# A mixture of experts: two sums of the experts' rows in DRAM in turn, an earlier place for their readback, one accumulation for the last two tiles, and the router in column halves

## The chip, the cores and the metric

The kernel runs on one core of a Trainium2 chip. A core has a matrix engine (TensorE, called PE in the profile), a vector engine (VectorE, DVE), a scalar engine (ScalarE, ACT), a general engine (GpSimd, POOL) and a synchronisation engine (SyncE, SP) that mostly issues transfers. Each has its own queue of instructions, worked off in order. Sixteen DMA engines move data between DRAM and the on-chip memory (SBUF); matmul results land in PSUM. The metric is the device time of one execution in microseconds.

## What is computed

512 tokens of 1024 numbers pass a first block (a state space branch and a pooling branch, then a mixture of experts) and a second block (a linear recurrent layer and differential attention). The change touches the mixture of experts alone:

```python
u2 = modulate(rmsnorm(h, norm_ffn_g), sh2, sc2)
h = h + g2[:, None, :] * moe_ffn(u2, ...)
# moe_ffn
scores = sigmoid(uf @ w_router)               # 512 x 64
choice = scores + router_bias                 # best 4 of 8 groups, then best 8 experts
wts = scores[top_e] / sum * 2.5
# every expert e on the tokens that chose it, and a shared expert on all:
#   (silu(u @ we_gate[e]) * (u @ we_up[e])) @ we_down[e], weighted, summed per token
```

All weights come from DRAM in 32 bits: 3 MB for one expert, 65 experts with the shared one.

## The kernel before

`moe` makes the block. The residual stream `hT` lies in SBUF with features in partitions. `modulated` norms it and makes eight operands u of 128x512 by a product on DVE (L325) and a scale and shift, on ACT (L329) or DVE (L331) in turn; `on_u` multiplies each with the router's weights into one PSUM tile (`logit`, L794); the rows of u are stored to DRAM as `u2_d`. `Routing.run` turns the logits (L855 to L859), picks the experts and sorts them by their counts.

`Schedule` then lists 52 tiles of 128 slots: four of the shared expert, 22 of one expert, 10 third tiles and 16 with two experts that take 64 columns each. `Experts.run` works through them. For a tile, POOL gathers 128 rows of `u2_d` by an indirect DMA (`fetch`, m_xg, L1164), PE turns them (L1179), multiplies gate and up (L1191), ACT and DVE make the hidden rows (m_hid), PE turns these (L1208, evicted to m_ht) and multiplies down (L1191, PSUM tag mm, three buffers). ACT and DVE evict the two halves with the weights of the slots into m_y (L1231, L1233; five buffers of 128x1024). For the shared tiles, a plain DMA writes m_y to `rt_d` (L1237); for others an indirect DMA adds its rows to `rt_d` by the token number (L1242), once for a tile of one expert, twice for one of two (index lists sgi and sgj): 66 such scatters. Since all add to one tensor, each waits until the last one has landed, and the buffer m_y is not free before. POOL issues gathers and scatters in one queue, in the order of the program.

SP issues the weights into m_we and m_wl (nine and six buffers of 1 MB), up to five experts ahead.

The last two tiles (`t.add`) aren't scattered. `parts` splits their rows in two float32r parts (L1258, L1259), `added` multiplies these by a one-hot matrix (`to`) into features by tokens (L1272, L1273), and `residual` (L1263) adds the product to `hT`. `back` reads `rt_d` when all scatters have landed (L1285, issued by SP), PE transposes it (L1290), and `residual` adds it. One `added` stands ahead of the last down product, the other after a loop over further blocks that these inputs don't need. There `on_h` feeds the sums of the next norm (`nsum`, L1424) as each part of `hT` is finished.

Of the kernel before, what the change touches and what calls it, by code (L numbers as in the profile page):

```python
# [166 lines left out]
class K:  # L167
# [142 lines left out]
    def modulated(self, pool, x, inv, gname, sh, sc, uh=None, ul=None, u_cb=None, rows=None, tile=None):  # L310
# [6 lines left out]
        for h in range(2):  # L317
# [5 lines left out]
            for k in range(4 * h, 4 * h + 4):  # L323
# [3 lines left out]
                if u_cb:  # L327
                    if k % 2:
                        nc.scalar.activation(u, u, AF.Identity, scale=a, bias=b)  # L329
                    else:  # L330
                        nc.vector.tensor_scalar(u, u, a, b, op0=OP.mult, op1=OP.add)  # L331
                    u_cb(k, u)
                    continue
# [428 lines left out]
def moe(g, hT, inv, on_h=None):  # L762
# [8 lines left out]
    rt_d = g.dram.tile([512, 1024], F32, name="rt_d")  # L771
    with contextlib.ExitStack() as st:
# [6 lines left out]
        with tc.tile_pool(name="head", bufs=1, reuse_waits="tile") as sp:  # L779
# [8 lines left out]
            with tc.tile_pool(name="route", bufs=1, reuse_waits="tile") as s3:  # L788
# [3 lines left out]
                def on_u(k, u):  # L792
                    us[k] = u
                    nc.tensor.matmul(logit[:64], lhsT=wr[:, k * 64:(k + 1) * 64], rhs=u, start=k == 0, stop=k == 7)  # L794
# [22 lines left out]
class Routing:  # L817


    def __init__(self, g, rp):  # L820
# [20 lines left out]
        nc.vector.tensor_scalar(self.half[:, 2:3], self.half[:, 0:1], 4096.0, None, op0=OP.mult)  # L841
        nc.gpsimd.memset(self.cap, 128.0)
# [3 lines left out]
    def run(self, sp, logit, rb, gc, store):  # L846
# [7 lines left out]
        lg = x[:64]  # L854
        nc.scalar.activation(lg, logit[:64], AF.Copy)  # L855
        p = sm()
        for c in range(4):
            first = nc.tensor.transpose(p[:, 64 * c:64 * c + 64], lg[:, c * P:(c + 1) * P], g.ident[:64, :64]).ins
# [261 lines left out]
class Experts:  # L1120
    def __init__(self, g, wp, lp, xp, u2_d, rt_d, hT):
        self.g, self.wp, self.lp, self.xp, self.u2_d, self.rt_d, self.hT = g, wp, lp, xp, u2_d, rt_d, hT
        self.raw, self.xg, self.us = {}, {}, []
# [28 lines left out]
    def begin(self):  # L1152

        self.raw = {i: self.load(e, i) for i, e in enumerate((64, 0, 1))}

# [65 lines left out]
    def out(self, tl, t):  # L1221
# [14 lines left out]
        if not tl.key:  # L1236
            nc.gpsimd.dma_start(out=self.rt_d[tl.b * P:tl.b * P + P], in_=y)  # L1237
        else:

            to = self.sl(tl.key)  # L1240
            for ix in (to[0],) if len(tl.ws) == 1 else (to[0][:64], to[2]):
                nc.gpsimd.indirect_dma_start(  # L1242
                    out=self.rt_d, out_offset=bass.IndirectOffsetOnAxis(ap=ix, axis=0), in_=y[:ix.shape[0]], in_offset=None,
                    bounds_check=511, oob_is_err=False, compute_op=OP.add)

    def parts(self, tl, t):
# [4 lines left out]
        to = self.tile("to", 512, 2, F32R)  # L1251
# [14 lines left out]
    def added(self, on_h=None):  # L1266

        yh, yl, to = self.add.pop(0)
        for m in range(8):
            p = self.g.acc()  # L1270
            s = slice(m * P, m * P + P)
            self.g.nc.tensor.matmul(p, lhsT=yh[:, s], rhs=to, start=True, stop=False)  # L1272
            self.g.nc.tensor.matmul(p, lhsT=yl[:, s], rhs=to, start=False, stop=True)  # L1273
# [6 lines left out]
    def back(self):  # L1280

        g, nc = self.g, self.g.nc
        tok = [self.x_tile().rearrange("p (c f) -> p c f", c=4) for q in range(4)]
        for q in range(4):
# [1179 lines left out]
```

## Time and profile before

| | us |
|---|---|
| median of 3 runs | 2569.54 (2568.93 to 2570.04) |
| profiled execution, its own time | 2574.54 |
| its span, from first to last instruction | 2572.8 |
| PE busy in the span | 2298.5 (89%) |
| DVE, ACT, POOL busy | 1308.7, 872.6, 759.6 |
| mean granted clock of PE | 0.949 |

Busy shares are means over stages that differ. A time in brackets behind a row is how long the engine sat idle before it, with an arrow to what it waited for. "L1242" is line 1242 of the kernel before. A tile's name stands without its buffer number: m_y is any of five buffers.

### The profile page before, as it was taken

The numbers are of one execution on the slowest core, as the hardware profiler recorded it, in microseconds if no ns is written. First come the engines' busy times: TensorE is split into PE (matmuls) and PEld (weight loads), VectorE is DVE, ScalarE is ACT, GpSimd is POOL, SyncE is SP. The second block draws the span as 40 slices with busy tenths as digits, with TensorE's granted clock in tenths as the row PEclk, the third lists the DMA queues.
The fourth block names the chain that finished last, engine by engine and source line by source line (L and its number), as shares of the span: only waits on it lengthen the run. The fifth ranks groups of instructions, "written<-read, shape, count | busy, mean of one in ns | idle before, by whom it ended". The sixth has DMA issues, their size and how long they took to land. (4 is left out here: it accounts for less than half of the span.)

```text
span 2572.8 us, 31633 instructions
## 1 busy us (share of the span) xinstructions
PE 2298.5 (89%) x11908; PEld 1646.4 (64%) x11908; DVE 1308.7 (51%) x2391; ACT 872.6 (34%) x1593; POOL 759.6 (30%) x589
## 2 busy tenths in 40 slices
PE   6899999998998999797888884898989999989997
PEld 2677888776885544333333333676778798888887
DVE  5666778658544433111111123858634557478765
ACT  3443433343222211111111111645315654345552
POOL 2333344013000121121212122538613311655212
PEclk9899999999998999899999996899989999999998
DMA  7223332345625799899899963376756342111221
GB/s 279 91 98 107 107 107 90 115 164 186 227 94 213 247 328 390 307 332 371 284 398 346 341 201 110 99 204 183 214 139 228 133 161 92 55 55 54 87 66 50
DMA packets 186602, 472.97 MB, mean 184 GB/s; under 512 B 62269, under 2 KB 113853, under 8 KB 146256
## 3 DMA queue, kind: packets, MB, share of 16 engines
q1 hardware_dynamic: 161392, 422.38, 45.9%
q0 software_dynamic: 15712, 35.12, 5.7%
q10 hardware_dynamic: 9344, 13.44, 1.7%
q8 instruction: 94, 1.54, 0.2%
q14 instruction: 60, 0.49, 0.1%
HBM read 421.56 MB, written 69.80 MB: 191 GB/s over the span
## 5 line engine op out<-in xcount | busy, mean ns | idle before, releaser
L224 POOL TENSOR_TENSOR wl<-wr,wh 128x1024 fp32r<-128x1024 f32 x80 | 203.7, 2562 | 384.7 <-ACT wh L223 382.1
L223 ACT ACTIVATE wh<-wr 128x1024 fp32r<-128x1024 f32 (+1 forms) x202 | 204.2, 1043 | 228.6 <-PE mm L205 147.2
L205 PE MATMUL mm<-uh,wh 128*128 128x512 f32 x640 | 258.7, 405 | 10.4 <-DVE cv L607 7.7
L205 PE MATMUL mm<-ul,wh 128*128 128x512 f32 x640 | 256.4, 401 | 0.0
L205 PE MATMUL mm<-uh,wl 128*128 128x512 f32 x640 | 255.7, 400 | 0.0
L205 PE MATMUL mm<-ya,wh 128*128 128x256 f32 x1280 | 242.8, 290 | 7.1 <-ACT wh L223 7.1
L1191 PE MATMUL mm<-m_we,m_x 128*64 128x512 f32 (+1 forms) x672 | 247.8, 599 | 0.0
L205 PEld LDWEIGHTS mm<-ya,wh 128*128 128x128 f32 x1280 | 203.8, 195 | 14.2 <-ACT wh L223 8.7
L224 DVE TENSOR_TENSOR wl<-wr,wh 128x1024 fp32r<-128x1024 f32 (+1 forms) x122 | 157.7, 1311 | 66.3 <-ACT wh L223 66.1
L205 PE MATMUL mm<-ya,wl 128*128 128x256 f32 x640 | 184.2, 288 | 0.0
L1191 PE MATMUL mm<-m_we,m_ht 128*64 128x512 f32 (+1 forms) x368 | 148.7, 621 | 28.0 <-ACT m_y L1231 23.4
L1191 PE MATMUL mm<-m_wl,m_x 128*64 128x512 f32 (+1 forms) x432 | 166.8, 598 | 2.9 <-DVE m_y L1233 1.8
L1242 POOL DMA_INDIRECT rt_d<-m_y,sgi x46 | 70.3, 1528 | 334.4 <-ACT m_y L1231 132.7
L1191 PEld LDWEIGHTS mm<-m_we,m_x 128*64 128x64 f32 (+1 forms) x672 | 86.7, 160 | 101.0 <-issue 99.6
L205 PEld LDWEIGHTS mm<-uh,wh 128*128 128x128 f32 x640 | 122.5, 191 | 41.6 <-issue 8.1
L1181 DVE COPY m_x<-sm 128x512 f32<-128x512 f32 x48 | 33.1, 690 | 223.2 <-PE mm L1191 171.0
L205 PEld LDWEIGHTS mm<-ul,wh 128*128 128x128 f32 x640 | 122.1, 191 | 29.1 <-issue 0.3
L205 PEld LDWEIGHTS mm<-uh,wl 128*128 128x128 f32 x640 | 121.9, 190 | 29.3
L205 PEld LDWEIGHTS mm<-ya,wl 128*128 128x128 f32 x640 | 124.7, 195 | 0.5
L1233 DVE TENSOR_SCALAR m_y<-mm,ssw 128x512 f32<-128x512 f32 x46 | 34.4, 749 | 162.4 <-DMA rt_d<-m_y,sgj 82.6
L1191 PE MATMUL mm<-m_wl,m_ht 128*64 128x512 f32 (+1 forms) x216 | 90.3, 634 | 28.6 <-ACT m_y L1231 20.0
L1191 PEld LDWEIGHTS mm<-m_wl,m_x 128*64 128x64 f32 (+1 forms) x432 | 57.7, 158 | 82.9 <-issue 76.2
(573 smaller groups left out, 4921.5 us busy)
## 6 DMA issues: line engine op xcount, KB each, us to landing
m_we<-in_w_exp_dram SPq DMA_DIRECT2D x117, 1024.0 KB
m_wl<-in_w_exp_dram SPq DMA_DIRECT2D x78, 1024.0 KB
wr<-in_w_grp_dram SPq DMA_DIRECT2D x32, 1024.0 KB
wr<-in_w_ada_dram SPq DMA_DIRECT2D x18, 1024.0 KB
ck<-pk_d SPq DMA_DIRECT2D x16, 1024.0 KB
csb<-cs_d ACTq DMA_DIRECT2D x16, 512.0 KB
wr<-in_w_pg_dram SPq DMA_DIRECT2D x8, 1024.0 KB
raw<-in_w_ada_dram SPq DMA_DIRECT2D x6, 1024.0 KB
```

The costliest lines, as they stand in the source:

```text
L205: nc.tensor.matmul(pt, lhsT=l, rhs=r, start=n == 0, stop=n == last)
L223: self.nc.scalar.activation(hi, src, AF.Copy)
L224: return (eng or self.nc.vector).tensor_sub(lo, src, hi.bitcast(F32)).ins
L1181: nc.vector.tensor_copy(x[:, 4:], v_(p, 4))
L1191: self.mark = self.g.nc.tensor.matmul(p[s], lhsT=x[:, s], rhs=w, start=start, stop=stop).ins
L1233: nc.vector.tensor_scalar(y[:, s], p, w, None, op0=OP.mult)
L1242: nc.gpsimd.indirect_dma_start(out=self.rt_d, out_offset=bass.IndirectOffsetOnAxis(ap=ix, axis=0), in_=y[:ix.shape[0]], in_offset=None, bo ...
```

## The change

The sum in DRAM becomes two, `rt_d[0]` and `rt_d[1]`, to which the scatters add in turn (`turn`); the shared tiles write the first, and `begin` clears the second from a zeroed m_y with four plain DMAs on POOL's queue. `back` reads both in two column halves (four transfers of 1 MB into m_we tiles), adds them with DVE and POOL, and then transposes; it stands ahead of the last tile's turn in the program. The `added` of the tile before the last is gone as a step of its own: `added(on_h)` accumulates both tiles, four matmuls for a part of 128 features instead of two. In the router all eight scales and shifts are ACT's, the logit product writes even k to partitions 0 to 63 and odd k to 64 to 127, and the four transposes of logits become matmuls with two identities on top of each other (`two`), which add the halves.

```diff
@@ modulated
-                    if k % 2:
-                        nc.scalar.activation(u, u, AF.Identity, scale=a, bias=b)
-                    else:
-                        nc.vector.tensor_scalar(u, u, a, b, op0=OP.mult, op1=OP.add)
+                    nc.scalar.activation(u, u, AF.Identity, scale=a, bias=b)
@@ moe
-    rt_d = g.dram.tile([512, 1024], F32, name="rt_d")
+    rt_d = [g.dram.tile([512, 1024], F32, name="rt_d%d" % i) for i in range(2)]
...
-                    nc.tensor.matmul(logit[:64], lhsT=wr[:, k * 64:(k + 1) * 64], rhs=u, start=k == 0, stop=k == 7)
+                    o = 64 * (k % 2)
+                    nc.tensor.matmul(logit[o:o + 64], lhsT=wr[:, k * 64:(k + 1) * 64], rhs=u, start=k < 2, stop=k > 5)
@@ Routing
+        self.two = t([P, 64], "two")
+        nc.vector.tensor_add(self.two, g.ident[:, :64], g.ident[:, 64:])
...
-        lg = x[:64]
-        nc.scalar.activation(lg, logit[:64], AF.Copy)
+        nc.scalar.activation(x, logit, AF.Copy)
         p = sm()
         for c in range(4):
-            first = nc.tensor.transpose(p[:, 64 * c:64 * c + 64], lg[:, c * P:(c + 1) * P], g.ident[:64, :64]).ins
+            first = nc.tensor.matmul(p[:, 64 * c:64 * c + 64], lhsT=x[:, c * P:(c + 1) * P], rhs=self.two, start=True,
+                                     stop=True).ins
@@ Experts.begin
+        zero = self.y()
+        self.g.nc.gpsimd.memset(zero, 0.0)
+        for b in range(4):
+            self.g.nc.gpsimd.dma_start(out=self.rt_d[1][b * P:b * P + P], in_=zero)
@@ Experts.out
-            nc.gpsimd.dma_start(out=self.rt_d[tl.b * P:tl.b * P + P], in_=y)
+            nc.gpsimd.dma_start(out=self.rt_d[0][tl.b * P:tl.b * P + P], in_=y)
...
+                self.turn ^= 1
                 nc.gpsimd.indirect_dma_start(
-                    out=self.rt_d, out_offset=bass.IndirectOffsetOnAxis(ap=ix, axis=0), in_=y[:ix.shape[0]], in_offset=None,
+                    out=self.rt_d[self.turn], out_offset=bass.IndirectOffsetOnAxis(ap=ix, axis=0), in_=y[:ix.shape[0]], in_offset=None,
@@ Experts.added
-        yh, yl, to = self.add.pop(0)
+        n = 2 * len(self.add)
...
-            self.g.nc.tensor.matmul(p, lhsT=yh[:, s], rhs=to, start=True, stop=False)
-            self.g.nc.tensor.matmul(p, lhsT=yl[:, s], rhs=to, start=False, stop=True)
+            for i, (y, to) in enumerate((y, to) for yh, yl, to in self.add for y in (yh, yl)):
+                self.g.nc.tensor.matmul(p, lhsT=y[:, s], rhs=to, start=i == 0, stop=i == n - 1)
@@ Experts.back
-        tok = [self.x_tile().rearrange("p (c f) -> p c f", c=4) for q in range(4)]
-        for q in range(4):
-            nc.sync.dma_start(out=tok[q], in_=self.rt_d[:, 256 * q:256 * q + 256].rearrange("(c p) f -> p c f", p=P))
+        tok = [[v_(self.w_tile(False), 4) for _ in range(2)] for q in range(2)]
+        for q in range(2):
+            for t, d in zip(tok[q], self.rt_d):
+                nc.sync.dma_start(out=t, in_=d[:, 512 * q:512 * q + 512].rearrange("(c p) f -> p c f", p=P))
         yield
+        for q, (t, t1) in enumerate(tok):
+            for j in range(2):
+                s = slice(256 * j, 256 * j + 256)
+                (nc.gpsimd if j else nc.vector).tensor_add(t[:, :, s], t[:, :, s], t1[:, :, s])
...
@@ Experts.run
+            if whole and i == N - 1:
+                drain(bk)
             t = self.turned(hid)
-            if whole and i == N - 1:
-                self.added()
             self.out(tl, t)
...
-        if whole:
-            with g.tc.issue_after(self.mark):
-                drain(bk)
```

The first place is POOL's queue at the end of the experts' loop. Before, `rt_d` is the one sum:

```order
119 L1242 DMA rt_d<-m_y,sgj 512x1024
120 L1242 DMA rt_d<-m_y,sgi 512x1024 x3
121 L1242 DMA rt_d<-m_y,sgj 512x1024
122 L1242 DMA rt_d<-m_y,sgi 512x1024
123 L1242 DMA rt_d<-m_y,sgj 512x1024
124 L1242 DMA rt_d<-m_y,sgi 512x1024
125 L1376 TENSOR_LOAD nextra
```

With the change, rt_d_5566 and rt_d_5567 are the two sums, and L1297 is their addition:

```order
146 L1248 DMA rt_d_5567<-m_y,sgi 512x1024
147 L1248 DMA rt_d_5566<-m_y,sgi 512x1024
148 L1248 DMA rt_d_5567<-m_y,sgj 512x1024
149 L1248 DMA rt_d_5566<-m_y,sgi 512x1024
150 L1248 DMA rt_d_5567<-m_y,sgj 512x1024
151 L1248 DMA rt_d_5566<-m_y,sgi 512x1024
152 L1297 TENSOR_TENSOR m_we<-m_we 128x4x256 x2
153 L1384 TENSOR_LOAD nextra
```

Before, every scatter of this list has the one ahead of it to wait for; with the change the neighbours are on different sums, and the semaphores of a scatter name the last one on its own sum. Two additions stand between the last scatter and the load of `nextra`.

The second place is PE's queue at the same end (mm<-m_wl,m_ht is the last down product, sm the transposes of what was read back). Before:

```order
3680 L1272 MATMUL mm<-m_to,m_y 128x512
3681 L1273 MATMUL mm<-m_to,m_y 128x512
3682 L1191 MATMUL mm<-m_wl,m_ht 128x512 x4
3683 L1290 MATMUL sm<-cst,m_xg 128x128 x32
3684 L1376 TENSOR_LOAD nextra
3685 L1378 COMPARE_AND_BRANCH
```

With the change (a is the turn of the last tile's hidden rows):

```order
3688 L1213 MATMUL a_9938<-cst,m_hid 128x128 x2
3689 L1196 MATMUL mm<-m_wl,m_ht 128x512 x4
3690 L1301 MATMUL sm<-cst,m_we 128x128 x32
3691 L1384 TENSOR_LOAD nextra
3692 L1386 COMPARE_AND_BRANCH
```

The one-hot matmuls ahead of the last down product, of which the last two rows are shown, are gone. The transposes stay behind that product and ahead of `nextra`.

The third place is POOL's queue at the start of the router (ri is the norm's factor). Before:

```order
51 L835 IOTA iota 128x128
52 L837 IOTA pid 128x1
53 L842 MEMSET cap 128x64
54 L947 MEMSET aux 128x64 x4
55 L948 MEMSET aux 128x4x64
56 L843 MEMSET cap 128x5
57 L844 MEMSET cap 128x37
58 L237 TENSOR_TENSOR ri<-rv,mhalf 128x4
```

With the change (m_y is the zeroed buffer):

```order
51 L1157 MEMSET m_y 128x1024
52 L834 IOTA iota 128x128
53 L836 IOTA pid 128x1
54 L843 MEMSET cap 128x64
55 L948 MEMSET aux 128x64 x4
56 L949 MEMSET aux 128x4x64
57 L1159 DMA rt_d_5567<-m_y 128x1024 x4
58 L844 MEMSET cap 128x5
59 L845 MEMSET cap 128x37
60 L237 TENSOR_TENSOR ri<-rv,mhalf 128x4
```

A memset of m_y leads the queue, and four transfers of zeros stand ahead of `ri`.

## Rows read from the trace of the kernel before

**Rows 1.** Stages by the table of windows: us, busy by engine, PEclk, DMA share, GB/s.
```profile
950.00:1000.00 50.00, 50.00 (x230) 21.56 (x228) 14.09 (x33) 7.78 (x16) 7.03 (x5) 1.00 1.02 396
1000.00:1500.00 500.00, 431.39 (x1608) 177.22 (x1603) 74.43 (x167) 65.28 (x137) 108.14 (x82) 0.96 0.92 341
1549.00:1582.00 33.00, 7.50 (x33) 6.55 (x32) 7.14 (x10) 1.27 (x2) 4.55 (x3) 0.59 0.33 82
```

**Rows 2.** Waits of PE, 838 to 1549 us: total us, times, longest.
```profile
PE mm L1191 <- ACT m_y L1231: 43.4, 16, 12.2
PE mm L1191 <- ACT m_ht L1210: 8.2, 3, 4.9
...
PE mm L1191 <- DMA m_wl<-in_w_exp_dram: 1.1, 2, 0.9
```

**Rows 3.** Tensor rt_d: issues (ns min/median/max, first and last), who waited, landing.
```profile
L1242 POOL DMA_INDIRECT rt_d<-m_y,sgi x46: 1418/1560/1873, 900.9 to 1562.4; - x46
...
L1237 POOL DMA_DIRECT2D rt_d<-m_y x4: 553/584/602, 853.7 to 888.7; - x4
...
  POOL rt_d L1242: 240.3, 38
...
DMA to landing us min/median/max: 3.1/8.3/19.1
```

**Rows 4.** Timeline of POOL, 1042 to 1069 us: start, us, what, idle before.
```profile
1042.91 1.03 POOL L1164 DMA_INDIRECT m_xg<-u_d,sgi  x1 [13.82 <-PE sm L1179]
...
1048.14 1.62 POOL L1242 DMA_INDIRECT rt_d<-m_y,sgi  x1 [0.30 <-issue]
1068.02 1.44 POOL L1242 DMA_INDIRECT rt_d<-m_y,sgi  x1 [18.27 <-ACT m_y L1231]
```

**Rows 5.** Timeline of PE, 1068 to 1076 us.
```profile
1068.08 5.76 PE L1191 MATMUL mm<-m_wl,m_ht 128*128 128x512 f32 x8 [12.19 <-ACT m_y L1231]
...
1074.87 3.60 PE L1191 MATMUL mm<-m_we,m_x 128*128 128x512 f32 x8
```

**Rows 6.** Timeline of all engines, 1518 to 1584 us.
```profile
1518.47 3.70 PE L1191 MATMUL mm<-m_we,m_ht 128*128 128x512 f32 x8
...
1525.85 0.69 ACT L1231 ACTIVATE m_y<-mm,ssw 128x512 f32<-128x512 f32 x1 [10.35 <-DMA rt_d<-m_y,sgj]
...
1533.26 1.56 POOL L1242 DMA_INDIRECT rt_d<-m_y,sgi  x1 [5.22 <-DMA rt_d<-m_y,sgi]
...
1545.51 3.67 PE L1191 MATMUL mm<-m_wl,m_ht 128*128 128x512 f32 x8
...
1568.62 2.15 SPq L1285 DMA_DIRECT2D m_xg<-rt_d  x4
...
1572.18 3.67 PE L1290 MATMUL sm<-cst,m_xg 128*128 128x128 f32 x16 [23.00 <-DMA m_xg<-rt_d]
...
1577.98 3.31 DVE L1263 SCALAR_TENSOR_TENSOR hT<-sm,mod,hT 128x512 f32<-128x512 f32 x4 [1.26 <-PE sm L1290]
...
1582.99 0.39 PE L1273 MATMUL mm<-m_to,m_y 128*128 128x512 f32 x1
...
1583.22 0.39 PE L1272 MATMUL mm<-m_to,m_y 128*128 128x512 f32 x1
```

**Rows 7.** Page, part 5, one kind of operation on POOL and DVE.
```profile
L224 POOL TENSOR_TENSOR wl<-wr,wh 128x1024 fp32r<-128x1024 f32 x80 | 203.7, 2562 | 384.7 <-ACT wh L223 382.1
...
L224 DVE TENSOR_TENSOR wl<-wr,wh 128x1024 fp32r<-128x1024 f32 (+1 forms) x122 | 157.7, 1311 | 66.3 <-ACT wh L223 66.1
```

**Rows 8.** Timeline of all engines, 804 to 815 us.
```profile
806.12 1.02 POOL L237 TENSOR_TENSOR ri<-rv,mhalf 128x4 f32<-128x4 f32 x1 [1.23 <-DVE rv L235]
...
809.72 0.81 ACT L329 ACTIVATE m_wl<-m_wl,mod,modAnorm_ffn 128x512 f32<-128x512 f32 x1 [5.67 <-DVE m_wl L325]
...
813.73 10.01 PE L794 MATMUL logit<-m_wl,wrt 128*64 128x512 f32 x16 [5.43 <-DVE m_wl L331]
```

**Rows 9.** Groups of instructions on POOL: busy, mean ns.
```profile
L1845 POOL MEMSET T<- 32x1024 f32 x2 | 1.9, 944 | 4.0 <-DMA o_d<-p_ei 4.0
```

More of the change, by code (lines that the diff above doesn't have):

```diff
@@ L1122, in __init__ @@
         self.g, self.wp, self.lp, self.xp, self.u2_d, self.rt_d, self.hT = g, wp, lp, xp, u2_d, rt_d, hT
-        self.raw, self.xg, self.us = {}, {}, []
+        self.raw, self.xg, self.us, self.turn = {}, {}, [], 0
     def tile(self, n, w, bufs, dt=F32):
@@ L1250, in parts @@
         yh, yl = ((self.y if tl.b is None else self.x_tile)(F32R) for _ in range(2))
-        to = self.tile("to", 512, 2, F32R)
+        to = self.tile("to", 512, 2, F32R) if tl.b is None else self.x_tile(F32R)[:, :512]
         tf = self.wp.tile([P, 1], F32, tag="m_tf", name="m_tf", bufs=1)
@@ L1289, in back @@
             for c in range(4):
-                nc.tensor.transpose(p[:, c * P:(c + 1) * P], tok[m // 2][:, c, (m % 2) * P:(m % 2) * P + P], g.ident)
+                nc.tensor.transpose(p[:, c * P:(c + 1) * P], tok[m // 4][0][:, c, (m % 4) * P:(m % 4) * P + P], g.ident)
             self.residual(m, p)
```

## Prediction

> **What bounds the kernel now.** I read the stage table first, then the waits of TensorE (PE), then the scatters one by one, then the end of the experts' loop. The stretch that the change touches runs from about 802 us (router) to 1600 us (last product of the block). In the stage table [rows 1] the reader sees three regimes. From 950 to 1000 PE is busy all the time and the DMA engines move 396 GB/s. From 1000 to 1500 PE is busy 431.39 of 500 us, so 68.6 us are idle, and the mean clock is 0.96; the DMA engines are busy 0.92 of it at 341 GB/s, so neither is the whole bound. From 1549 to 1582 PE works 7.50 of 33 us at a granted clock of 0.59: there something else sets the end.
>
> What PE waits for in the loop [rows 2]: 43.4 us in 16 waits for ScalarE's (ACT's) eviction of a finished down product into m_y, the longest 12.2 us, and 8.2 us for m_ht, which stands behind such an eviction in ACT's queue. Weights (m_wl) cost 1.1 us. So the loop isn't held by its weights. An eviction waits because its m_y buffer, one of five, has not been scattered yet: 66 scatters stand on one tensor, each waits for the one before it, and GpSimd (POOL) sits 240.3 us in 38 such waits; a scatter lands 8.3 us after its issue in the median, 19.1 at most [rows 3]. The longest stall shows how [rows 4]: the scatter of 1048.14 goes out behind four gathers that began at 1042.91, the next scatter comes at 1068.02, and PE, idle for 12.19 us, resumes at 1068.08, slowly: eight matmul rows in 5.76 us where the same eight take 3.60 shortly after [rows 5].
>
> The end of the loop is the same chain without cover [rows 6]. The down product of the third last tile is done at 1518.47 + 3.70 = 1522.2, but its eviction starts only at 1525.85, after a wait of 10.35 us. The scatters of this time take 6.78 us each (1.56 at the one of 1533.26, behind 5.22 us of waiting for the one before), and the readback, which needs all of them, issues at 1568.62. PE transposes from 1572.18, after 23.00 us idle, and the last residual on VectorE (DVE) ends at 1577.98 + 3.31 = 1581.3.
>
> **The change, part by part.** I make the sum against the profiled execution's 2574.54 us; it lies 5.0 us above the median of the runs, and I take 5.0 off at the end.
>
> *Two sums in the loop.* The order of the instructions shows that scatters alternate between two tensors and that each waits only for the last one on its own. A chain of 66 becomes two of 33. The 240.3 us of POOL's waiting don't vanish, but PE sees only what reaches the five buffers: 43.4 + 8.2 = 51.6 us. The price of a scatter with another in flight isn't in the trace. Bounds: a lone one in the tail, where the DMA share is 0.33, takes 6.78 us, and 8.3 is the median of all; the five transfers between 1042.91 and 1068.02 took 25.1 us together, 5.0 each, while weights were loading. If two in flight each land twice as late, the pace stays at one in 6.78 to 8.3; if each lands as when alone, it is half of that. I take about 5, nearest to the row of five under load. The loop needs one scatter per 10 us on average ((1562.4 - 900.9)/65 between the first and last [rows 3]), two per tile where a tile has two experts; 8.3 falls behind there and 5 doesn't, so the backlog goes except where POOL itself stands behind a gather. What would hold the loop then is the DMA engines: a share of 0.92 leaves 0.08 x 500 = 40 us. The bytes at the rate of 950 to 1000 give 341 x 500 / 396 = 431 us, so at best 69. I take 4/5 of the 40: **-32**, bounds 0 and -52 (all of the 51.6). The matmuls slowed after a stall (2.16 us in [rows 5]) come back with the stalls; I count nothing extra for them and keep that as a reserve against new waits for weights.
>
> *The readback.* Without a backlog the third last tile's eviction starts at about 1522.3, ends at 1523.0, and its scatter lands 6.78 to 8.3 us later, at 1530 to 1531.3, instead of 1568.6. Take 1531. The readback is now four transfers of 1 MB instead of 0.5. Before, first transposes came 3.56 us after the issue of the first 0.5 MB; the first pair is 1.5 MB more, 4.0 us at 396 GB/s, so 1538.6; the second pair 5.3 us later, 1543.9. Each pair is added by DVE and POOL halves: POOL's 128x1024 at 2.56 us, DVE's at 1.31 [rows 7], side by side, so 2.56: 1546.5. The last 16 transposes take 3.67 and the last residual, 3.31/4, follows them: 1551.0. The end moves from 1581.3 to 1551.0, **-30**. PE's own queue is out of the way by then: even if the last down product stayed at 1545.51 + 3.67 = 1549.2, it would be done, and it moves up, since sixteen accumulation matmuls ahead of it go. Bounds: -10, if the chain still lags by three scatters, to -32.
>
> The Trainium skill (SBUF — State Buffer, section "Who interferes with whom") says that a DVE instruction with two SBUF inputs contends with a GpSimd instruction that reads SBUF. By that the two halves of an add would run one after the other, 1.31 + 2.56, and the readback would end 1.3 us later; no row of before shows the two side by side on one tile, so I leave it as a bound.
>
> *The last two tiles in one accumulation.* Removed: sixteen matmuls and eight residuals before the last down product, in time in which the chain was waited for, so worth 0 here. Added: sixteen matmuls in the final accumulation, which nothing covers; its rows stand 0.23 us apart (1582.99, 1583.22 [rows 6]): **+3.7**, up to 5.3 where the residual and the clock slow it, down to 2 where DVE was the slower one anyway.
>
> *Router.* The logit product starts at 813.73, because PE waits for a scale and shift on DVE, and runs 10.01 us [rows 8]. ACT makes the second operand from 809.72 on in 0.81 us; with all eight on ACT the other six follow, and the last is there at 809.72 + 7 x 0.81 = 815.4; the last matmul pair, 10.01/8, ends at 816.7 instead of 823.7: -7.0. Against it: POOL's queue gets a memset and four transfers ahead of `ri`, on which the norm waits: 0.94 us by the nearest row (32x1024), and 4 x 0.584 [rows 3, 9], 3.3 us, of which 1.23 is the wait that `ri` had anyway: +2.1. If the column halves don't run side by side, 10.01 us from about 809.7 + 2.1 on end at 821.8, only -1.9. The zeros are 2 MB in the stretch in which the first experts load, at most 5.3 us. I take **-3**, bounds -5 and +4. That the transposes of the logits become matmuls with a stacked identity is four small matmuls for four: 0.
>
> Sum: -32 - 30 + 3.7 - 3 = **-61**. 2574.5 - 61 = 2513.5 profiled, **2508.5** as a median.
>
> **The rivals.** *Only the end gains.* The DMA engines at 0.92 already hold the loop: scatters come earlier, loads then start earlier and collide, and the stalls return under m_wl or m_xg. Then -30 + 3.7 - 3 = -29: 2540. For it: the share of 1.02 and the full PE just before 1000 [rows 1]. Against: weights cost PE 1.1 us in all [rows 2].
>
> *Everything gains.* All 51.6 us go, with some of the slow matmuls behind them; the readback at its best, the router too: -52 - 32 + 3 - 5 = -86: 2484. For it: 396 GB/s beside a full PE.
>
> *Slower.* Two scatters in flight share the engines and each lands at 13.6 us or later: twice the lone 6.78 is the point from which it decides. The pace stays, the last scatter lands where it did, and the readback pays 2 MB more (5.3), the adds (2.56) and the longer accumulation (3.7), less 3 of the router: +8.6: 2578. For it: the 19.9 us that one scatter took behind four gathers [rows 4]. Against: five transfers in that time, so they overlapped.
>
> The Trainium skill (DMA: Bandwidth & Descriptors, section "Issuing engines are not separate DMA queues") speaks for this rival's mechanism: transfers issued concurrently run on the same 16 engines and interleave, so that issuing more of them saves no transfer time. By it the pace would gain only where a scatter's time is latency and not bytes; the rows of the lone scatters, at a DMA share of 0.33 [rows 1], say that much of the 6.78 us is not bytes.
>
> **How the numbers follow.** Forecast 0.53 (its own range 2492 to 2528), only the end 0.24, everything 0.12, slower or nothing 0.11. The range 2484 to 2547 holds the forecast, nearly all of "only the end" and half of "everything"; outside are the slower case and the far side of the best. Times of the rivals are medians. A change of 0.2% (5 us) is about what can be told from none. Faster 0.88, within 0.2% 0.04, slower 0.08.
>
> **What would show it.** In the changed kernel: POOL's waits for scatters under 120 us in all, PE's waits for m_y under 15 us in the loop, PE idle from 1000 to 1500 near 35 us and the DMA share near 0.98. The readback's first issue within 12 us of the third last tile's down product, and the last readback transposes some 20 us after it. The final accumulation some 4 us longer, the logit product finished about 3 us earlier relative to the last product of the stage before. The prediction is wrong if median landing of a scatter rises to 13 us or more, if PE's waits reappear at about the same size under the weights, or if the readback is held by something other than scatters, such as free m_we buffers or the weight transfers in front of it in SP's queue. The instructions that were reordered in the second block carry no term; if that stretch moves by more than 5 us, a cause is missing here.

## The result and the profile after

The changed kernel takes **2510.71 us** (median of 4 runs, 2504.29 to 2511.93) beside 2569.79 of the kernel before on the same chip: a ratio of 0.9762, interval 0.9742 to 0.9782. The forecast was 2508.5. The two profiled executions lie further apart than the medians: that of after is the fastest of its runs (2504.29, span 2502.5), that of before (2574.54) is slower than all of its own, so their spans differ by 70.3 us and the medians by 59. The sum below is made on the spans.

I cut both spans at five marks and take the length of each stage, in us:

| stage | before | after | difference | forecast |
|---|---|---|---|---|
| start to the last product ahead of the router | 802.6 | 797.3 | -5.3 | 0 |
| to the first gate/up product | 23.1 | 18.1 | -5.0 | -3 |
| to the start of the third last tile's down product | 692.7 | 646.4 | -46.3 | -32 |
| to the end of the last residual of the readback | 62.8 | 41.2 | -21.6 | -30 |
| to the start of the norm's factor (`nrm`) | 17.5 | 18.5 | +1.0 | +3.7 |
| to the end of the program | 974.0 | 981.0 | +7.0 | 0 |

The first row is not put down to the change: PE's order is the same there, and over the executions of the kernels below that mark lies anywhere from 795.2 to 802.4 us. Without it, -64.9 stands against the forecast's -61.

**The loop.** The table of windows of the kernel before, over the whole stage, and of the kernel after, over the stage and over a stretch of 450 us in its middle (columns as in [rows 1]):

```profile
825.74:1518.47 692.73, 620.72 (x2430) 266.60 (x2428) 144.74 (x389) 105.27 (x213) 141.69 (x110) 0.97 0.90 334
```

```profile
815.36:1461.75 646.39, 615.40 (x2441) 263.97 (x2439) 145.25 (x389) 105.47 (x213) 149.24 (x114) 0.99 0.97 366
988.00:1438.00 450.00, 420.68 (x1600) 171.90 (x1597) 74.93 (x167) 65.08 (x136) 108.66 (x81) 0.99 0.99 377
```

PE's idle time falls from 692.73 - 620.72 = 72.0 to 646.39 - 615.40 = 31.0: 41.0 us. The other 5.3 are PE's own work, which is done at a clock of 0.99 instead of 0.97. The DMA engines now move 366 GB/s instead of 334, and are busy 0.99 of the middle stretch. The waits of PE in the loop, to be held against [rows 2]:

```profile
PE mm L1196 <- ACT m_y L1236: 10.2, 10, 1.1
PE mm L1196 <- DVE m_hid L1206: 6.4, 6, 1.1
PE mm L1196 <- DMA m_wl<-in_w_exp_dram: 5.9, 1, 5.9
```

The wait for an eviction fell from 43.4 us (longest 12.2) to 10.2 (longest 1.1). One wait for weights of 5.9 us is new; the change's second profile has it too (6.0). The tensor of the sums, against [rows 3]:

```profile
L1248 POOL DMA_INDIRECT rt_d<-m_y,sgi x46: 1411/1557/2134, 889.5 to 1475.2; - x46
...
L1292 SPq DMA_DIRECT2D m_we<-rt_d x4: 392/470/847, 1481.2 to 1482.7; - x4
...
  POOL rt_d L1248: 90.8, 23
...
DMA to landing us min/median/max: 5.8/10.6/22.5
```

POOL sits 90.8 us behind scatters instead of 240.3. The median landing rose from 8.3 to 10.6 us, not to the 16.6 that two in flight would take if they only shared the time.

**The end of the loop.** The timelines of the kernel after: first POOL's scatters from 1459 us on, then rows of all engines up to the last accumulation (against [rows 6]):

```profile
1459.08 1.43 POOL L1248 DMA_INDIRECT rt_d<-m_y,sgi  x1 [2.21 <-ACT m_ht L1215]
1466.87 1.56 POOL L1248 DMA_INDIRECT rt_d<-m_y,sgj  x1 [6.36 <-DMA rt_d<-m_y,sgi]
1468.73 1.43 POOL L1248 DMA_INDIRECT rt_d<-m_y,sgi  x1 [0.30 <-issue]
1473.30 1.57 POOL L1248 DMA_INDIRECT rt_d<-m_y,sgj  x1 [3.13 <-DMA rt_d<-m_y,sgj]
1475.17 1.56 POOL L1248 DMA_INDIRECT rt_d<-m_y,sgi  x1 [0.30 <-ACT m_y L1264]
```

```profile
1461.75 3.70 PE L1196 MATMUL mm<-m_we,m_ht 128*128 128x512 f32 x8
...
1481.16 2.38 SPq L1292 DMA_DIRECT2D m_we<-rt_d  x4
...
1489.88 1.22 DVE L1297 TENSOR_TENSOR m_we<-m_we 128x1024 f32<-128x1024 f32 x1 [7.49 <-DMA m_we<-rt_d]
1489.90 3.41 POOL L1297 TENSOR_TENSOR m_we<-m_we 128x1024 f32<-128x1024 f32 x1 [13.18 <-DMA m_we<-rt_d]
...
1494.98 2.34 POOL L1297 TENSOR_TENSOR m_we<-m_we 128x1024 f32<-128x1024 f32 x1 [1.67 <-DMA m_we<-rt_d]
1496.05 2.36 DVE L1297 TENSOR_TENSOR m_we<-m_we 128x1024 f32<-128x1024 f32 x1
...
1498.51 3.65 PE L1301 MATMUL sm<-cst,m_we 128*128 128x128 f32 x16 [3.17 <-issue]
1499.64 3.31 DVE L1269 SCALAR_TENSOR_TENSOR hT<-sm,mod,hT 128x512 f32<-128x512 f32 x4 [1.23 <-PE sm L1301]
```

The third last tile's down product ends at 1461.75 + 3.70 = 1465.45, and its scatter, the last, goes out only at 1475.17: three older ones, of the two tiles before it, still stand ahead of it, and two of the four wait 6.36 and 3.13 us for another. The readback issues at 1481.16, and its last residual ends at 1499.64 + 3.31 = 1502.95.

### The profile page after: what moved, and what is told of

Read it like the earlier page. It is cut to its first block, busy times and chain, and to the rows that moved or that the text cites. A ratio compares the mean times of both kernels' runs of the same rounds, so it can differ in the third digit from the quotient of the medians.

```text
span 2502.5 us, 31640 instructions
## 1 busy us (share of the span) xinstructions
PE 2283.3 (91%) x11912; PEld 1641.4 (66%) x11912; DVE 1308.8 (52%) x2382; ACT 876.6 (35%) x1597; POOL 771.3 (31%) x596
## 5 line engine op out<-in xcount | busy, mean ns | idle before, releaser
L1196 PE MATMUL mm<-m_we,m_ht 128*64 128x512 f32 (+1 forms) x368 | 140.8, 601 | 11.4 <-ACT m_y L1236 6.7
L205 PEld LDWEIGHTS mm<-uh,wl 128*128 128x128 f32 x640 | 121.7, 190 | 29.3
L1169 POOL DMA_INDIRECT m_xg<-u_d,sgi x48 | 50.4, 1050 | 273.5 <-PE sm L1184 81.1
L1522 PE MATMUL mm<-xh,wh 128*128 128x512 f32 x256 | 106.3, 418 | 5.7 <-ACT xh L223 3.4
L1522 PE MATMUL mm<-xl,wh 128*128 128x512 f32 x256 | 105.6, 413 | 4.0 <-DVE xl L224 2.8
```

What stands on the lines that cost most here:

```text
L205: nc.tensor.matmul(pt, lhsT=l, rhs=r, start=n == 0, stop=n == last)
L1169: self.g.nc.gpsimd.indirect_dma_start(out=xg, out_offset=None, in_=self.u2_d, bounds_check=511, oob_is_err=False, in_offset=bass.IndirectO ...
L1196: self.mark = self.g.nc.tensor.matmul(p[s], lhsT=x[:, s], rhs=w, start=start, stop=stop).ins
L1522: nc.tensor.matmul(p, lhsT=a_[:, s], rhs=b_, start=k == 0 and i == 0, stop=k == 7 and i == 2)
```

## The experiments

Each kernel's profile is one execution; medians and ratios are to the kernel before on the same chip. "The change" is the changed kernel, and every edit is made to it. The first four kernels ran together on one chip, then four, two and two on others; there the kernel before took 2569.18 to 2574.45 us, so between the groups the ratios are compared and not the times.

**The change again.**

> The changed kernel again, as the common measure of this group. Expected: 2505 to 2512 us, about 59 us below the kernel before; the first 797 us, whose order on PE did not change, vary by some 5 us between executions and are not the change's.

Measured: 2506.06 us, 0.9744 (0.9719 to 0.9769); from the last product ahead of the router on, the profiled stages agree with those above within 0.8 us each. What follows is held against this run; single rows of the change are shown from the first profile.

**One sum for all scatters, the rest as changed.**

```
             for ix in (to[0],) if len(tl.ws) == 1 else (to[0][:64], to[2]):
-                self.turn ^= 1
                 nc.gpsimd.indirect_dma_start(
```

> The changed kernel with every scatter on the first sum again (the second is still cleared, read and added). Theory (two chains instead of one carry the gain in the loop, about 46 us, and let the readback start early, about 20 more): the loop is back where it was, the last scatter too, and the 4 MB readback, the adds and the longer last accumulation now cost without a gain: 2575 to 2585 us, POOL's waits for scatters over 220 us, PE's waits for m_y near 43 us. Rival (the gain is the end's: earlier place of the readback, no accumulation ahead of the last down product): below 2550 us.

Measured: 2587.17 us, 1.0054 (1.0036 to 1.0072): half a percent slower than before, and 2 us above the theory's range. From its waits of PE in the loop, and from the rows of the sums:

```profile
PE mm L1196 <- ACT m_y L1236: 40.6, 13, 10.8
```

```profile
L1291 SPq DMA_DIRECT2D m_we<-rt_d x4: 392/470/665, 1562.3 to 1563.9; - x4
...
  POOL rt_d L1247: 239.7, 35
```

All three signs of before are back: the waits for m_y (43.4 before), POOL's waits (240.3) and the readback issued behind a chain that runs on to 1562.3. From the first gate/up product to the third last tile's down product it takes 698.7 us where the change takes 646.2, and from there to the last residual of the readback 65.1 instead of 41.3. So the gain of some 81 us beside the change comes from the chain being cut in two: 52 of it in the loop and 24 at the end. The other parts, without the two chains, cost 14 us more than before (1.0054): that is the "slower" case of the forecast (2578 us there), reached by taking the mechanism away.

**The router of before.** DVE again makes every second operand, the logits come in one sum of 64 rows, and four transposes turn them:

```
-                    nc.scalar.activation(u, u, AF.Identity, scale=a, bias=b)
+                    if k % 2:
+                        nc.scalar.activation(u, u, AF.Identity, scale=a, bias=b)
+                    else:
+                        nc.vector.tensor_scalar(u, u, a, b, op0=OP.mult, op1=OP.add)
...
-                    o = 64 * (k % 2)
-                    nc.tensor.matmul(logit[o:o + 64], lhsT=wr[:, k * 64:(k + 1) * 64], rhs=u, start=k < 2, stop=k > 5)
+                    nc.tensor.matmul(logit[:64], lhsT=wr[:, k * 64:(k + 1) * 64], rhs=u, start=k == 0, stop=k == 7)
...
```

> The changed kernel with the router of before (scales and shifts on ACT and DVE in turn, one logit product of 64 rows, four transposes). Theory (the router's part is worth the 5.5 us by which the logits ended earlier behind the last product before them): 2514 to 2517 us. Rival (what the router gains is waited for again before the first experts' tile): 2510 to 2512 us.

Measured: 2511.43 us, 0.9762 (0.9736 to 0.9787), whose interval overlaps that of the change. The time lies in the rival's range, but both ranges were set before the change's repeat came out at 2506.06, so it doesn't decide. The profile is sharper: first PE's logit row of the change, then that of this kernel.

```profile
803.81 1.11 PE L240 MATMUL sm<-cst,ri 128*128 128x128 f32 x4 [3.33 <-POOL ri L237]
...
806.56 6.30 PE L793 MATMUL logit<-m_wl,wrt 128*64 128x512 f32 x16 [1.63 <-ACT m_wl L328]
```

```profile
805.83 1.12 PE L240 MATMUL sm<-cst,ri 128*128 128x128 f32 x4 [3.33 <-POOL ri L237]
...
812.36 9.15 PE L795 MATMUL logit<-m_wl,wrt 128*64 128x512 f32 x16 [5.42 <-DVE m_wl L331]
```

From the L240 product, the same in both, the logits come 812.36 - 805.83 = 6.5 us after it instead of 2.75, and take 9.15 instead of 6.30. The new router brings the first gate/up product forward by 6.4 us in the profiles (24.2 - 17.8 from the same mark); at the readback's last residual 4.6 of it are left, and the time of the runs shows 5, within the noise.

**The accumulation split, first tile's part behind the turn.**

```
...
+            if whole and i == N - 1:
+                self.added(k=1)
             self.out(tl, t)
```

Here `added(k=1)` accumulates the first of the two tiles by itself, and the last `added(on_h)` only the second.

> The changed kernel with the two last tiles accumulated apart again: sixteen matmuls and eight residuals of the tile before the last stand ahead of the last down product, the last accumulation has two matmuls per part. Theory (nothing covers the longer last accumulation, and it holds m_y's space so long that the next block's first weights come late): 4 to 7 us faster than the change, 2504 to 2507 us, and no wait of the first weights' issue for the accumulation. Rival (the sixteen matmuls and eight residuals now delay the readback's transposes, since the chain no longer covers them): the same or up to 4 us slower.

Measured: 2511.15 us, 0.9756 (0.9731 to 0.9782). It didn't test what it was made for: the scheduler mixed the parts with the readback's transposes and set the last down product at 1507.33, behind both, where the change has it at 1477.18. It shows nothing on the split, beyond no gain.

**Half of the scatters left out.**

```
                 self.turn ^= 1
+                if self.turn:
+                    continue
```

> The changed kernel without the 33 scatters on the second sum (these rows are left out of the result; all else, the gathers, products, evictions and the readback, stays). Theory (with two chains the scatters bind nothing more in the loop, which now runs at PE's own pace and at the weights' transfer): the loop gains at most 5 us, the end some 7 by which its last scatters still lag, together 2495 to 2506 us, PE's waits for m_y unchanged near 10 us. Rival (two chains still hold the loop, or the scatters' traffic does): 2480 us or less.

Measured: 2505.73 us, 0.9742 (0.9711 to 0.9773), no less than the change. The same 450 us in the table of windows, its largest wait of PE, and POOL's waits for scatters:

```profile
988.00:1438.00 450.00, 431.89 (x1647) 177.95 (x1646) 76.01 (x160) 67.77 (x140) 66.62 (x53) 0.99 0.95 370
```

```profile
PE sm L1184 <- DMA m_xg<-u_d,sgi: 12.4, 5, 5.3
```

```profile
  POOL rt_d L1250: 81.1, 12
```

The 33 scatters that are left are one chain again, and POOL still sits 81.1 us in 12 waits for one of them. PE gains 11 us of work in this stretch (431.89 against 420.68), the last scatter goes out 8.5 us earlier, and what PE then waits for is gathers. The loop as a whole gains less: 640.3 us to the third last tile's down product instead of 646.2, and 2.7 us more at the end. Behind the last residual it takes 5.1 us longer (1003.8 instead of 998.7), and in the time the gain isn't seen. So all that half of the scatters still cost the loop, by waiting and by traffic together, is about 6 us in these profiles.

**The split with its first part ahead of the readback.** The same edit as in the split above, but the call stands ahead of `drain(bk)`.

> The changed kernel with the tile before the last accumulated by itself ahead of the readback's part in the program, so that its sixteen matmuls and eight residuals run while the readback is waited for. Theory (the longer last accumulation costs what it adds there, 3 to 5 us, and holds up the next block's first weights, which now wait 6.3 us for it): 4 to 8 us faster than the change, 2499 to 2503 us beside 2506. Rival (the last accumulation is paced by the sums of the next norm and DVE anyway, and the weights come late for another reason): within 2 us of the change.

Measured: 2505.05 us, 0.9726 (0.9701 to 0.9750), not separable from the change. Two windows inside the last accumulation and the norm's sums (`nsum`), the change first, then this kernel, with one row of these sums each:

```profile
1512.00:1516.00 4.00, 4.00 (x32) 3.74 (x31) 1.12 (x2) 1.27 (x2) 0.00 (x0) 1.00 0.48 201
...
1511.42 0.95 PE L1432 MATMUL nsum<-ngain,m_xg 128*128 128x2 f32 x8
```

```profile
1511.00:1515.00 4.00, 4.00 (x20) 3.81 (x18) 1.56 (x3) 1.93 (x4) 0.00 (x0) 0.50 0.64 229
...
1513.38 1.70 PE L1434 MATMUL nsum<-ngain,m_xg 128*128 128x2 f32 x8
```

Sixteen accumulation products were saved at the end, and the stretch from the last residual to `nrm` grew from 18.5 to 22.5 us: eight products of the norm's sums take 1.70 us at a granted clock of 0.50 (1.2 GHz) instead of 0.95 at 1.00 (2.4 GHz). The next block's first weights (L1613 in the change) were asked for 5.9 us after the last residual, as in before, instead of 14.3; both together are nothing in the time. Whether the fewer products are why the clock fell is taken up with the last two kernels.

**The readback in quarters, added on DVE.**

```
-        for q in range(2):
+        for q in range(4):
...
-                (nc.gpsimd if j else nc.vector).tensor_add(t[:, :, s], t[:, :, s], t1[:, :, s])
+                nc.vector.tensor_add(t[:, :, s], t[:, :, s], t1[:, :, s])
```

> The changed kernel with the readback in eight transfers of 0.5 MB (quarters of the columns of each sum) and all additions on DVE. Theory (behind the last transfer stand an addition of half a tile on two engines that hold each other up, 2.4 us, sixteen transposes and four residuals; with quarters it is one addition of 1.3, eight transposes and two residuals): the last residual some 3 us earlier, 2502 to 2504 us beside 2506. Rival (the eight transfers cost as much more in issue and landing): the same.

Measured: 2504.46 us, 0.9733 (0.9708 to 0.9757). The readback takes 19.7 us from issue to its last residual instead of 21.8, each DVE add 1.22 us. The next stretch gives it back: 23.7 instead of 18.5 us to `nrm`, at a granted clock of 0.67 from 1505 to 1525.

**The zeros later.** The clearing of the second sum moves from the start of the experts' setup to the end of the router's operand store, as a call of its own (`ex.clear()`).

> The changed kernel with the clearing of the second sum (memset and four transfers) behind the norm's factor in POOL's queue, after the logits. Theory (PE waits 3.3 us for the factor in the changed kernel against 1.4 before, and the path from there to the first experts' tile has no slack): 2 us faster, 2504 us beside 2506. Rival (the path has slack, or the zeros now delay the rows or the gathers that follow): 2505 to 2509 us.

Measured: 2507.95 us, 0.9744 (0.9720 to 0.9769). PE's product with `ri` (L240 in the change) ends 5.7 us after the last product ahead of the router instead of 7.7, so the first gate/up product comes 1.9 us earlier, as worked out; in the time it isn't seen.

**PE kept busy while it waits for the readback.** Ten products of 128x512 into an accumulator that nobody reads:

```
+            if whole and i == N - 1:
+                with g.tc.issue_after(self.mark):
+                    p = g.acc()
+                    for _ in range(10):
...
```

> The changed kernel with ten more 128x512 products behind the last down product, whose result nobody reads: they fill PE's idle 10 us before the transposes of the readback. Theory (PE is idle there and its granted clock is 0.50 through the transposes and until the last accumulation; if PE stays busy the clock stays at 1.00, so the transposes and the first products of the accumulation take half the time): the granted clock between the readback's issue and the last residual is near 1.00, the time from the readback's issue to the next norm's factor falls by 2 to 5 us, 2501 to 2504 us. Rival (that stretch is paced by transfers and DVE, whatever PE's clock): the clock rises and the time stays within 1 us of the change's 2506.

Measured: 2500.45 us, 0.9737 (0.9714 to 0.9761). From PE's timeline:

```profile
1482.64 8.75 PE L1349 MATMUL mm<-m_wl,m_ht 128*128 128x512 f32 x20
1492.02 1.09 PE L1301 MATMUL sm<-cst,m_we 128*128 128x128 f32 x8 [0.64 <-DVE m_we L1297]
```

The granted clock is 1.00 from the readback's issue up to these rows, and 0.71 from there to the last residual, where the change has 0.50. The first transposes take 1.09 us where the change takes 1.97, but the readback 21.1 instead of 21.8, and from its issue to the norm's factor it is 39.7 us instead of the 40.1 of the change's repeat. So this much more clock is worth under 1 us in the stretch. The median of 2500.45 looks like the theory's, but the ratio can't be told from the change's.

**Busy, quarters and late zeros together** (seven products instead of ten).

> Three edits on the changed kernel together: seven products that nobody reads behind the last down product, the readback in quarters with DVE's additions, and the clearing behind the norm's factor. Theory (each shortens its own stretch: 2.0 us at the router and 2.2 at the readback, as the traces of the single edits showed, and 2 to 5 by the clock; what quarters gained was lost again to a granted clock of 0.50 in the accumulation, which busy PE now keeps up): 2497 to 2501 us. Rival (what the stretches gain is lost behind them, since the next block's first weights arrive no earlier): 2503 us or more.

Measured: 2508.42 us, 0.9763 (0.9744 to 0.9782): the rival's range; the gains don't add up to one that can be measured.

**The early split with the clock held.** As the early split, with two more products per part, which the next ones overwrite:

```
...
+            if k is None and on_h:
+                for y, to in ((y, to) for yh, yl, to in add for y in (yh, yl)):
+                    self.g.nc.tensor.matmul(p, lhsT=y[:, s], rhs=to, start=True, stop=True)
```

> The tile before the last accumulated by itself ahead of the readback, as in the run before of that kind, and ahead of each part of the last accumulation two products whose result is overwritten, so that PE does as many products there as in the changed kernel while the first tile's m_y buffers are free long before. Theory (splitting alone lost by PE's clock: with eight parts of two products the granted clock was 0.50 and the norm's sums took 1.70 us instead of 0.95; the first weights' issue 6 us after the last residual instead of 14 is worth the 4 us between the norm's factor and its use): from the last residual to the norm's factor 18 to 19 us as in the changed kernel and from there to its use about 3 instead of 7.4, 2500 to 2503 us. Rival (the clock in the last accumulation follows what PE did while it waited for the readback, so it is 0.50 here too): 22 us or more from the last residual to the factor, 2504 us or more.

Measured: 2508.91 us, 0.9754 (0.9731 to 0.9777). The time and the stretch are those of the rival, but not for its reason: with as many products at the end as the change has, the clock rose to 1.00 and then fell. The windows from 1510 us on:

```profile
1510.00:1514.00 4.00, 4.00 (x30) 3.66 (x29) 1.86 (x3) 1.69 (x3) 0.00 (x0) 1.00 0.63 256
1514.00:1518.00 4.00, 4.00 (x23) 3.78 (x24) 0.33 (x1) 0.63 (x1) 0.00 (x0) 0.70 0.47 141
1518.00:1522.00 4.00, 4.00 (x17) 3.52 (x15) 1.50 (x2) 1.67 (x3) 0.00 (x0) 0.50 0.08 33
```

So the way to `nrm` stays at 22.9 us, although the first weights are asked for 8.0 us after the last residual.

**That and the late zeros.**

> The same with the clearing of the second sum behind the norm's factor in POOL's queue, which took 2.0 us from the router in the trace of that edit alone. Theory (the router's 2 us reach the end): 2498 to 2501 us, 2 us below the run beside it. Rival (they are waited for again or lie within what varies between executions): the same as the run beside it.

Measured: 2511.6 us, 0.9760 (0.9737 to 0.9783): no gain either. But its profile answers the run beside it. The instructions from the readback on are the same, and here the clock stays up:

```profile
1513.00:1517.00 4.00, 4.00 (x30) 3.66 (x29) 1.88 (x3) 1.70 (x3) 0.00 (x0) 1.00 0.63 254
1517.00:1521.00 4.00, 4.00 (x29) 3.64 (x29) 1.07 (x2) 0.67 (x2) 0.00 (x0) 1.00 0.49 143
```

The way to `nrm` is 18.6 us, 4.3 less. So two executions of the same end can differ by as much as the early split seemed to lose by its clock, and the number of products alone doesn't set the clock.

No version beats the change by more than its interval: the best ratio, 0.9726 of the early split, lies inside the interval of the change itself.

## Why the prediction came out right, step by step

That the total came within 2 us is partly luck. The loop gave 14.3 us more than its term, the router 2.0 and the last accumulation 2.7; the readback gave 8.4 less, and the second block cost 7.0 that no term had. These nearly cancel.

**Loop: -46.3 where -32 was forecast.** The mechanism is shown: undoing the alternation alone brings the waits, the chain and more than the old time back. The size was taken as 4/5 of the DMA engines' spare share (40 us), and the factor 4/5 came from no row: PE's idle time fell by 41.0. The share was not a hard bound either, since the rate in the middle rose to 377 GB/s at a share of 0.99, where the share alone would have let 341 go to 341 x 0.99 / 0.92 = 367. The 5.3 us of faster matmuls, which were kept as a reserve against new waits for weights, came on top; the one new wait, of 5.9 us, is already within the idle time. The loop's signposts stood as set: POOL's waits under 120, m_y under 15, share near 0.98; PE's idle time in the middle, 29.3 of 450, is 32.6 on 500, where 35 was given. That the scatters no longer hold most of the loop is shown by leaving half of them out. What does is not separated: PE's own work is 615.4 of the 646.4 us, and the DMA engines are busy 0.97 of it.

One reading was off without changing the sum: the lone scatter of 6.78 us stands at 1526 to 1533, where the DMA share is 0.28, and not in the window of 0.33.

The Trainium skill (DMA: Bandwidth & Descriptors, section "Issuing engines are not separate DMA queues") had spoken for the slower rival, since concurrent transfers interleave on the same engines. The scatters did land later, in 10.6 instead of 8.3 us, but with one chain and half of the scatters the median is 10.1 too, so little of it comes from the second chain. And two chains at 10.6 give one scatter in 5.3 us, near the 5 that was taken from the five transfers under load.

**Readback: -21.6 where -30 was forecast.** Two parts of the step were too small. From the end of the third last down product to the issue the forecast had 1531 - 1522.2 = 8.8 us; it was 15.7, because its scatter wasn't the next one: three scatters of the two tiles before stood ahead. "Without a backlog" was true of the loop on the whole, not of this moment, and the sign set for it, an issue within 12 us, was missed. From the issue to the last residual it had 1551 - 1531 = 20.0 us; it was 21.8. The first pair was added 8.72 us after the issue instead of 7.6, the second pair 5.1 later as worked out (5.3), and the last adds cost about 0.9 more than the 2.56: DVE began its half at 1496.05, behind residuals, and needed 2.36 us beside POOL's 2.34, where it needs 1.22 at 1489.88; POOL's first half took 3.41. 6.9 + 1.8 are the 8.7 us between the 30.3 worked out and 21.6.

So the rule that was kept as a bound holds here (the Trainium skill, SBUF — State Buffer, section "Who interferes with whom"): a DVE instruction with two SBUF inputs contends with one of GpSimd that reads SBUF. By it the end was to come 1.3 us later; the rows show about 0.9, since DVE's last half ended 1.09 us behind POOL's, which took 2.34 where 2.56 was reckoned.

**The last accumulation: +1.0 where +3.7 was forecast.** The sixteen products cost more than the term, and the price comes back behind them. The last part of `hT` and the sums that follow it, before, then after:

```profile
1590.13 7.67 PE L1424 MATMUL nsum<-ngain,m_xg 128*128 128x2 f32 x40
1590.33 0.75 DVE L1263 SCALAR_TENSOR_TENSOR hT<-mm,mod,hT 128x512 f32<-128x512 f32 x1 [0.60 <-PE mm L1273]
```

```profile
1517.78 2.73 PE L1432 MATMUL nsum<-ngain,m_xg 128*128 128x2 f32 x24
1517.98 0.75 DVE L1269 SCALAR_TENSOR_TENSOR hT<-mm,mod,hT 128x512 f32<-128x512 f32 x1 [0.18 <-PE mm L1279]
```

The last part is done 15.8 us after the readback's last residual instead of 9.8: 6.0 us, above the 5.3 that was given as the most. But the sums end 1.8 us after it instead of 6.7, since 24 products are left instead of 40 and the granted clock is 1.00, where before it was 0.51 from 1591 to 1598. 6.0 - 4.9 is the 1.0 measured to within 0.1. The prediction had no term for the sums. How much of the 4.9 will come again is open, since the clock of this stretch differs between executions of the same instructions (18.6 and 22.9 us in the last two kernels).

**Router: -5.0 where -3 was forecast**, at the end of the given bounds. The working had -7.0 for the logits and +2.1 for POOL's queue, and was cut to -3 in case the column halves don't run side by side. They do: the same sixteen products take 6.30 us instead of 10.01 [rows 8], at a lower mean clock. Before, then after:

```profile
813.73:823.74 10.01, 10.01 (x16) 2.76 (x16) 1.31 (x3) 0.33 (x1) 0.00 (x0) 0.70 1.01 418
```

```profile
806.56:812.86 6.30, 6.29 (x16) 2.47 (x16) 3.28 (x6) 4.88 (x7) 0.00 (x0) 0.63 1.02 425
```

With the router of before, the first gate/up product comes 6.4 us later, and moving the zeros away brings 1.9, so both terms had their size.

**The second block: +7.0 where 0 was forecast.** The text had said that a cause is missing if this moves by over 5 us, and it is. One is in the trace: DVE waits 4.29 us for a weight of the next block in front of the norm's own work, so `nrm` to hT takes 7.3 us instead of 3.2. SP's queue ahead of that transfer, in before, then in the change with the wait for it (h_d is a store of `hT`):

```profile
1591.11 0.33 SPq L1426 DMA_DIRECT2D h_d<-hT  x1
1591.48 0.76 SPq L1609 DMA_DIRECT2D wr<-in_w_l_dram  x1
```

```profile
1518.76 0.35 SPq L1434 DMA_DIRECT2D h_d<-hT  x1
1519.16 0.42 SPq L1617 DMA_DIRECT2D wr<-in_w_l_dram  x1
...
1525.61 1.29 DVE L1623 TENSOR_TENSOR wr<-wr,vecs 128x512 f32<-128x512 f32 x2 [4.29 <-DMA wr<-in_w_l_dram]
```

```profile
  DVE wr L1623: 4.3, 1
```

The last fence is who waited for L1617. This transfer stands behind the second store of `hT`, which needs the last part that the longer accumulation makes. So it goes out 16.2 us after the readback's last residual instead of 10.2: the 6.0 us of the accumulation come back here. Two other transfers of weights, those of L1613, wait 6.3 us for the accumulation's products (L1279) and go out at 14.3 instead of 5.9; but only ACT waited for them, 2.6 us as in before. The early split tells them apart: those of L1613 are back at 5.9, while that of L1617 stays at 16.2, and from the last residual to the norm's use in `hT` it is 25.7 us, as in the change (25.8; before 20.7). DVE doesn't wait there, since `nrm` itself comes 4 us later.

The total isn't settled by it: from the last residual to the end the change takes 999.5 us and that of before 991.5 in its one profile, while the other kernels lie from 997.4 (the early split) to 1007.0 (busy, quarters and late zeros). The late weight explains some 4 us of the 7; how the rest divides between PE's clock, the order of the instructions and mere spread is open.

## What to carry to other kernels

A chain of dependent transfers on one tensor is worth cutting in two where most of a link is latency: read it from the lone links (6.78 us here at a DMA share of 0.28) and from the share of the DMA engines that is left. Here the gain in PE's idle time, 41.0 us, was about what that share left, 40, and the faster matmuls came on top. At the end of the loop, count the links that are still queued when the last work is done. And where work at the end of a stage gets longer, ask which store of its result stands in a queue ahead of the next stage's loads.

## What the runs showed that was not expected

- A scatter with no other in flight is hardly faster under the weights: with half of them left out, and the rest in one chain, the median landing of the scatters' line alone is 10.1 us, beside 10.7 in the change and 8.4 before. So most of the rise is there without the second chain. The DMA engines are busier in both (0.95 and 0.99 from 988 to 1438 us; in before 0.92 from 1000 to 1500); that this is the cause is not shown.
- PE was granted 0.50 in stretches in which it was busy all the time (4.00 of 4.00 us, from 1511 to 1515 and again to 1519, in the early split), and the change, which runs sixteen accumulation products more there, was granted 1.00. But with those products put back, one profile fell to 0.50 and another of the same instructions stayed at 1.00: 22.9 and 18.6 us to `nrm`. One profile can't price an edit there to better than some 4 us.
- POOL's 128x1024 add took 3.41 us beside a DVE add of 1.22 that was over after a third of it, and 2.34 beside one of 2.36 that began 1.07 us later. In these two pairs, and in both of the change's second profile, the engine that started later was the one that was held up.
